# Two transformer blocks on one core: four projection chunks begin on single K tiles, group two of K is taken in two halves, and table products are merged

## The chip, the cores and the metric

The kernel runs on 1 core of a Trainium2 chip. The metric is the device time of one execution in microseconds (us). Before the change it is 1740.43 us, the median of 3 runs (1739.6 to 1742.21). The engines that matter here are TensorE (PE; its weight loads are shown apart as PEld), VectorE (DVE), ScalarE (ACT) and SyncE (SP), which issues nearly all transfers.

## The reference

Batch 1, 256 tokens, model width 2048, all in float32. Two blocks run one after the other. Only the beginning of the first concerns the change:

```
mod = silu(c) @ w_ada + b_ada                     # 2048 -> 6*2048: shift, scale, gate, twice
h   = rms_norm(x, g_attn) * (1 + sc_a) + sh_a
proj = h @ w_in                                   # 2048 -> 7632 columns, split into q, k, v, index, latent, gates
qa, ka, qi, ki, mq, mk get a rotary embedding: t1*cos - t2*sin, t2*cos + t1*sin
...                                               # sparse and dense attention, merge, gated convolution FFN
second block: pooled windows, a grouped product, a gate, an output projection, a final norm
```

Before the rotation of `qa`, `ka`, `mq` and `mk` the vectors are scaled by gains, so that the kernel folds the gains into the cosine and sine tables once.

## The kernel before

**The products.** Every large product runs in float32 split in two parts: a weight tile `raw` (512 KB, two K tiles of 128 rows by 512 columns) is loaded, ACT writes its rounded part (line 157, `SC.copy`), DVE writes the remainder (line 79, `tt(lo, src, hi, OP.subtract)`), and PE adds three products per K tile and half of the tokens (line 378): high by high, high by low, low by high. One such unit is 12 matmuls of 512 columns. There are 6 `raw` buffers (`NRAW`) and 5 split buffers `hl` (`NHL`), so that a load waits until the unit six before it has been used up.

**The modulation.** `silu(c) @ w_ada` is not a matmul: each 512 KB tile of `w_ada` is multiplied by the broadcast `c` and summed along the row on DVE (line 175, called a job here). Jobs wait in a list, and `pump(n)` emits the next n of them. A K tile of 128 rows of `h` needs four jobs (its shift and its scale, in two halves each) before its `A1` and `SH1` exist.

**The input projection** has 15 chunks of 512 columns (the first, `MISC`, of 400; `QI0`, `QI1` stay in PSUM, the `keep` tiles). Since the modulation comes tile by tile, K is cut in groups of K tiles, `groups = [(0, 2), (2, 6), (6, 10), (10, 16)]`. For each group all 15 chunks are taken in turn and added to partial sums `pacc`: copied by ACT in the first group (line 426), added by DVE later. Between two chunks the jobs of the next group are emitted at a rate of 1.05 times what is needed; three chunks before the end of a group the list is emptied up to that group (`pump_to`) and `prep1` makes the next `hT`: ACT applies scale and shift, ACT and DVE split the result.

**The head** (lines 289 to 340) is written in a `manual_schedule`, that is, its instructions stand on each engine in the order of the code: load `c` and the four `xT`, squares of `xT` and their folds, the inverse root, its broadcast `rB0`, 30 small matmuls without use (`warm`), all 8 jobs of the first group, the split of the first weight unit, `prep1(0)`, the other three `xT` norms. What comes after the head is put in order by the scheduler of the framework; each engine then works its list strictly in that order.

**The tables** (lines 448 to 490): some twenty small DVE operations on the angles `ang`, two sines on ACT, and 16 products of `cs` and `sn` with the gains `grow` (`tqa`, `tka`, `tqm`, `tkm`).

Of the kernel before, what the change touches and what calls it, by code (L numbers as in the profile page):

```python
# [29 lines left out]
def block_pair_kernel(ctx: ExitStack, tc: tile.TileContext, T: dict, out: bass.AP):  # L30
# [187 lines left out]
    def job_group(g):  # L218
        k0, k1 = groups[g]
# [40 lines left out]
    def prep1(g):  # L260
        k0, k1 = groups[g]
# [27 lines left out]
    with tc.manual_schedule(engines={ET.SP, ET.DVE, ET.Activation, ET.PE}):  # L289
# [29 lines left out]
        job_group(0)  # L319
# [18 lines left out]
        prep1(0)  # L338
# [27 lines left out]
    def gemm_gen(st, W, k0, nk, evac, rate=0.0, tail=0, head=0, kw=None, n=512, pre=(), ps=None,  # L366
# [32 lines left out]
        for a in late:  # L399
# [5 lines left out]
    w1 = {i: (T["w_misc"] if i == MISC else T["w_in"][i - 1]) for i in range(15)}  # L405
    n1 = {i: (NMISC if i == MISC else 512) for i in range(15)}
    acc = {}

    keep = {QI0: [ps_tp([128, 512], name="keep") for _ in range(2)],
            QI1: [ps_at([128, 512], name="keep") for _ in range(2)]}  # L410
    for i in range(7):
        if i not in keep:
            acc[i] = s4([128, 2, 512], name=f"pacc{i}")
# [20 lines left out]
    for g in range(1, NG + 1):  # L434
        job_group(g)
    for g in range(NG):
        k0, k1 = groups[g]
        for i in range(nch[g]):
            if g == 0 and i >= 7:
                acc[i] = s4([128, 2, 512], name=f"pacc{i}")  # L440
            gemm(st1, w1[i], k0, k1 - k0, evac1(i, g), n=n1[i], rate=rates[g],
                 pre=[unit0] if g == 0 and i == MISC else [], ps=keep.get(i), part=(g == 0 or i not in keep, i not in keep))
            if i == nch[g] - 3:
                pump_to(4 * sum(size[g + 2:]))
                prep1(g + 1)
        if g == 0:
# [35 lines left out]
            def folded(o, n, f0, name):  # L482

                r = const([128, 4, 2, n], name=name)
                for q, (tab, go) in enumerate(((cs, 0), (sn, n), (cs, n), (sn, 0))):
                    gb = grow[:, None, o + go:o + go + n].to_broadcast([128, 2, n])
                    tt(r[:, q], tab[:, :, f0:f0 + n], gb, OP.mult)
                return r
            tqa, tka = folded(0, 16, 0, "tqa"), folded(32, 16, 0, "tka")
            tqm, tkm = folded(64, 32, 24, "tqm"), folded(128, 32, 24, "tkm")  # L490
# [189 lines left out]
    def rope_a(a, H, tab):  # L680
        v = heads(a, H)
        rope(v[:, :, :, 0:16], v[:, :, :, 16:32], [tab[:, q] for q in range(4)], H, 16)
# [115 lines left out]
    rope(kr[:, :, :, 0:32], kr[:, :, :, 32:64], [tkm[:, q] for q in range(4)], 1, 32)  # L798
# [7 lines left out]
    for j in range(4):  # L806
        qv = mq[j].rearrange("p t (h d) -> p t h d", d=192)
        kv = mkv[j].rearrange("p t (h d) -> p t h d", d=256)
        rope(qv[:, :, :, 128:160], qv[:, :, :, 160:192], [tqm[:, q] for q in range(4)], 2, 32)
# [496 lines left out]
```

## Time and profile before

| | |
|---|---|
| Median of 3 runs | 1740.43 us |
| The profiled execution | 1743.09 us, its span 1741.3 us |
| PE busy | 1692.9 us, 97% of the span |
| DVE busy | 1369.1 us, 79% |
| ACT busy | 910.8 us, 52% |
| Granted TensorE clock, mean | 0.989 of full speed |
| DMA | 455.59 MB, mean 262 GB/s |
| `raw` from `w_ada`, `w_in`: issue to landing, median | 4.8, 5.1 us |

Busy time of PE says only that a matmul was under way; how many it finished is read from the counts. The share over the whole span hides the beginning: PE has its gaps there, and from about 96 us on there are hardly any until the end of the projection. So the stretches of the first 165 us are read one by one: first PE's gaps, then, for each gap, what the engine before it was doing and for whom that one waited.

### The profile page before, as it was taken

The numbers are of one execution on the slowest core, as the hardware profiler recorded it, in microseconds if no ns is written. First come the engines' busy times: TensorE is split into PE (matmuls) and PEld (weight loads), VectorE is DVE, ScalarE is ACT, GpSimd is POOL, SyncE is SP. The second block draws the span as 40 slices with busy tenths as digits, with TensorE's granted clock in tenths as the row PEclk, the third lists the DMA queues.
The fourth block names the chain that finished last, engine by engine and source line by source line (L and its number), as shares of the span: only waits on it lengthen the run. The fifth ranks groups of instructions, "written<-read, shape, count | busy, mean of one in ns | idle before, by whom it ended". The sixth has DMA issues, their size and how long they took to land.

```text
span 1741.3 us, 22010 instructions
## 1 busy us (share of the span) xinstructions
PE 1692.9 (97%) x7786; PEld 1385.5 (80%) x7786; DVE 1369.1 (79%) x2079; ACT 910.8 (52%) x1283; POOL 4.2 (0%) x15
## 2 busy tenths in 40 slices
PE   8899999999999989999999999999999999999997
PEld 6688888878778868788888788887888777888886
DVE  8899999998978767599677676777877777766765
ACT  4644354767854456555455544555345565454443
POOL 0000000000000000000000000000000000000000
PEclk9999999999999999999999999999999999999999
DMA  8999988588868868677877787777777748778762
GB/s 324 342 333 324 339 324 278 191 295 295 277 224 323 287 206 313 214 242 238 296 247 251 232 268 261 260 245 261 272 255 252 248 160 269 255 254 277 238 201 94
DMA packets 127495, 455.59 MB, mean 262 GB/s; under 512 B 14357, under 2 KB 15893, under 8 KB 127385
## 3 DMA queue, kind: packets, MB, share of 16 engines
q1 hardware_dynamic: 127384, 454.19, 77.0%
q8 instruction: 61, 1.00, 0.2%
q14 instruction: 50, 0.40, 0.1%
HBM read 452.04 MB, written 2.10 MB: 261 GB/s over the span
## 4 chain that ended last, share of the span: by engine, by line
PE 59%; DMA 18%; DVE 14%; issue 5%; ACT 3%; SPq 0%; DVEq 0%; ACTq 0%
PE mm L378 51%; DMA raw<-in_w_mod 13%; DVE hl L79 5%; DMA raw<-in_w_ada 4%; DVE raw L175 3%; PE keep L378 2%; ACT hl L157 1%; PE mm L1171 1%; DVE cv L1031 1%; PE tp L1025 1%; DVE score L599 1%; DVE cv L1033 0%; DVE pacc L79 0%; PE tp L922 0%; DMA cst<-in_cst 0%
## 5 line engine op out<-in xcount | busy, mean ns | idle before, releaser
L157 ACT CAST hl<-raw 128x1024 fp32r<-128x1024 f32 (+2 forms) x564 | 586.6, 1046 | 584.5 <-PE mm L378 432.0
L79 DVE TENSOR_TENSOR hl<-raw,hl 128x1024 fp32r<-128x1024 f32 (+2 forms) x564 | 675.7, 1212 | 141.5 <-ACT hl L157 140.8
L378 PE MATMUL mm<-hl,hN 128*128 128x512 f32 x2880 | 676.4, 394 | 6.6 <-DVE hN L79 2.4
L378 PEld LDWEIGHTS mm<-hl,hN 128*128 128x128 f32 x2880 | 540.8, 190 | 121.3 <-DVE hN L79 4.0
L175 DVE SCALAR_TENSOR_TENSOR raw<-raw,cB 128x1024 f32<-128x1024 f32 x288 | 350.5, 1220 | 184.7 <-DMA raw<-in_w_mod 139.9
L378 PE MATMUL mm<-hl,hT 128*128 128x512 f32 (+1 forms) x1248 | 290.9, 392 | 8.0 <-ACT hT L157 3.3
L378 PEld LDWEIGHTS mm<-hl,hT 128*128 128x128 f32 x1248 | 234.2, 190 | 56.5 <-ACT hl L157 4.1
L378 PE MATMUL mm<-hl,gThi 128*128 128x512 f32 x704 | 219.9, 395 | 6.2 <-DVE hl L79 3.4
L378 PEld LDWEIGHTS mm<-hl,gThi 128*128 128x128 f32 x704 | 132.9, 190 | 35.9 <-DVE hl L79 5.0
L378 PE MATMUL mm<-hl,gTlo 128*128 128x512 f32 x352 | 137.8, 395 | 0.0
L378 PE MATMUL mm<-hl,pair 128*128 128x512 f32 x384 | 89.5, 392 | 0.0
L378 PE MATMUL mm<-hl,zT 128*128 128x512 f32 x384 | 87.5, 389 | 0.0
L378 PEld LDWEIGHTS mm<-hl,zT 128*128 128x128 f32 x384 | 71.9, 188 | 14.8
L378 PEld LDWEIGHTS mm<-hl,pair 128*128 128x128 f32 x384 | 71.5, 188 | 14.6
L378 PEld LDWEIGHTS mm<-hl,gTlo 128*128 128x128 f32 x352 | 66.9, 190 | 13.8 <-DVE gTlo L79 0.2
L1029 ACT ACTIVATE cv<-tp,wcv 128x256 f32<-128x256 f32 x88 | 44.9, 562 | 47.9 <-DVE cv L1033 39.4
L79 DVE TENSOR_TENSOR pacc<-pacc,mm 128x512 f32<-128x512 f32 (+1 forms) x78 | 52.2, 671 | 6.8 <-PE mm L378 6.3
L378 PE MATMUL mm<-hl,oaT 128*128 128x512 f32 x192 | 48.0, 399 | 0.0
L378 PE MATMUL mm<-hl,obT 128*128 128x512 f32 x192 | 47.1, 397 | 0.6 <-DVE obT L79 0.6
L378 PE MATMUL keep<-hl,hT 128*128 128x512 f32 x192 | 45.7, 395 | 0.8 <-DVE hl L79 0.8
L378 PEld LDWEIGHTS keep<-hl,hT 128*128 128x128 f32 x192 | 36.5, 191 | 9.0 <-DVE hl L79 1.6
L378 PEld LDWEIGHTS mm<-hl,obT 128*128 128x128 f32 x192 | 35.1, 188 | 8.0 <-DVE obT L79 1.0
(331 smaller groups left out, 1191.1 us busy)
## 6 DMA issues: line engine op xcount, KB each, us to landing
raw<-in_w_ada SPq DMA_DIRECT2D x192, 512.0 KB, 4.8
raw<-in_w_up SPq DMA_DIRECT2D x176, 512.0 KB, 4.6
raw<-in_w_in SPq DMA_DIRECT2D x112, 512.0 KB, 5.1
raw<-in_w_mod SPq DMA_DIRECT2D x96, 512.0 KB, 4.5
raw<-in_w_down SPq DMA_DIRECT2D x88, 512.0 KB, 4.6
raw<-in_pool_w_in SPq DMA_DIRECT2D x64, 512.0 KB, 4.5
raw<-in_w_o SPq DMA_DIRECT2D x32, 512.0 KB, 4.9
raw<-in_pool_w_out SPq DMA_DIRECT2D x32, 512.0 KB, 4.3
```

Source lines behind the costliest of these rows:

```text
L79: return V.tensor_tensor(o, a, b, op=op)
L157: SC.copy(hi, src)
L175: V.scalar_tensor_tensor(raw, raw, 1.0, cact[cv][h], op0=OP.mult, op1=OP.mult, accum_out=acc)
L378: PE.matmul(ps[t][:, :n], lhsT=st(k0 + k, t, a), rhs=hl[b][:, i, :], start=(part[0] and k == 0 and x == 0), stop=(part[1] and k == nk - 1 ...
L599: V.scalar_tensor_tensor(score, r[:, i, :], w, score, op0=OP.mult, op1=OP.add)
L1025: PE.transpose(p[:, i, t * 128:(t + 1) * 128], u[:, t, f * 128:(f + 1) * 128], ident)
L1029: SC.activation(cv[:, f, :], p[:, i, :], AF.Identity, bias=wcv[:, 3, fi:fi + 1], scale=wcv[:, 2, fi:fi + 1])
L1031: V.scalar_tensor_tensor(cv[:, f, 1:], p[:, i, :255], wcv[:, 1, fi:fi + 1], cv[:, f, 1:], op0=OP.mult, op1=OP.add)
L1171: PE.matmul(pv[:, q, :], lhsT=hls[k // 2][wa][:, k % 2, f * 128:(f + 1) * 128], rhs=pooled[i][xb][:, k, :], start=(k == 0 and x == 0), sto ...
```

## The change

- **Head, order of loads.** The first K group, tiles (0, 2), is taken tile by tile by the chunks 0 to 3. Four jobs (tile 0) are emitted, then half of the first weight unit is loaded (`load_half`, 205 or 262 KB, each in a `raw` buffer of its own), `hT` is made for one tile (`prep_half`), and 6 matmuls follow (`mm_half`), the same for chunk 1, two jobs, chunks 2 and 3, two jobs; then the second tile with its four halves. The four chunks hold their PSUM tiles meanwhile (two pairs of `mm`, two of `keep`). ACT copies the sums of chunk 0 between the matmuls of chunk 0 and the split for chunk 1. `colB`, `grow`, `posi` and `wcv` are loaded after all eight halves.
- **Second group in halves.** Jobs of tiles (2, 4) and (4, 6) are separate groups, with a `fin` (four small DVE operations) each. Chunks 4 to 14 take K tiles (0, 2) as before, with 1.53 jobs per unit; then chunks 0 to 3 take (2, 4) with their sums kept in PSUM, `prep1(4, 6)`, the same chunks take (4, 6) in the order 0, 3, 1, 2, and chunks 4 to 14 take (2, 6).
- **Tables.** The 16 products become 4, of 128 and 256 columns.
- **Squares.** The squares of `xT[0]` and `xT[2]` go from DVE to ACT.

```diff
-        q[0]()
-        tt(xsq[0], xT[0], xT[0], OP.mult)
-        fold(0)
-        SC.activation(xsq[1], xT[1], AF.Square)
...
+        for c in range(3):
+            q[c]()
+            SC.activation(xsq[c], xT[c], AF.Square)
+            fold(c)
...
-        job_group(0)
+        for k in range(2):
+            job_group(k, k + 1)
         pump(WU[0])
...
         warm(ones, WU[1])
-        pump(WU[2])
+        pump(1)
         norm_x(0)
-        pump(WU[3])
-        unit0 = load_split(T["w_misc"][0], NMISC)
-        pump(1000)
+        pump(2)
...
+        def load_half(c, i):
+            n = n1[c]
+            raw = raw_tile()
+            nc.sync.dma_start(raw[:, :n], w1[c][0][:, i * n:(i + 1) * n])
...
+            split(hl0[c][:, 0, i, :n], hl0[c][:, 1, i, :n], raw[:, :n])
...
+        load_half(0, 0)
+        prep_half(0)
+        mm_half(0, 0)
+        load_half(1, 0)
+        mm_half(1, 0)
+        pump(2)
+        for c in range(2, 4):
+            load_half(c, 0)
+            mm_half(c, 0)
+        pump(2)
+        load_half(0, 1)
+        prep_half(1)
...
+        for c in range(4):
+            if c > 0:
+                load_half(c, 1)
+            mm_half(c, 1)
+            if c not in keep:
+                for t in range(2):
+                    SC.copy(acc[c][:, t, :n1[c]], ps0[c][t][:, :n1[c]])
         nc.sync.dma_start(colB, T["pcol"][:, 48:COL_N])
...
-        prep1(0)
...
-    for g in range(1, NG + 1):
-        job_group(g)
+
+    for k0, k1 in ((2, 4), (4, 6), *groups[2:]):
+        job_group(k0, k1)
+    rates[0] = RG * 4 * size[1] / (nch[0] - 4)
...
+        if g == 1:
...
+            for i in range(4):
+                gemm(st1, w1[i], 2, 2, lambda t, p: None, n=n1[i], rate=rates[1], ps=ps1[i], part=(i not in keep, False))
+            prep1(4, 6)
+            for i in (0, 3, 1, 2):
+                gemm(st1, w1[i], 4, 2, evac1(i, 1), n=n1[i], rate=rates[1], ps=ps1[i], part=(False, i not in keep))
+        for i in range(done, nch[g]):
```

**What stands where now.** On ACT before, in the second half of the first group: `hl_450` is the split of the unit after the chunk whose sums are in `mm_418`, `mm_419`.

```order
L157 CAST hl_422<-raw_420 128x1024
L426 COPY pacc_72_392<-mm_393 128x512
L426 COPY pacc_72_392<-mm_394 128x512
L426 COPY pacc_78_417<-mm_418 128x512
L426 COPY pacc_78_417<-mm_419 128x512
L157 CAST hl_450<-raw_448 128x1024
L157 CAST hl_475<-raw_473 128x1024
```

The split `hl_450` stands behind the copy of the sums of the chunk just before it; `hl_475` stands ahead of the copies of its own predecessor. On ACT after, in the same part of the program (`hl_498`, `hl_551` and `hl_595` are the units of the chunks summed in `mm_494`, `mm_547` and the next):

```order
L457 COPY pacc_88_460<-mm_461 128x512
L457 COPY pacc_88_460<-mm_462 128x512
L157 CAST hl_498<-raw_496 128x1024
L255 ACTIVATE h_119_585<-xT_92,SH_74,A_73 128x256 x2
L157 CAST hl_523<-raw_521 128x1024
L457 COPY pacc_96_493<-mm_494 128x512
L457 COPY pacc_96_493<-mm_495 128x512
L457 COPY pacc_102_518<-mm_519 128x512
L457 COPY pacc_102_518<-mm_520 128x512
L157 CAST hl_551<-raw_549 128x1024
L457 COPY pacc_109_546<-mm_547 128x512
L157 CAST hT_584<-h_119_585 128x512
```

Two splits in these rows stand behind the copies of the chunk just before them, and two rows further on `hl_595` does, behind the copy of `mm_548`. On DVE before, between the third last and the second last unit of the first group (`raw`, `vs` are jobs; `SH`, `A` the shift and scale made from them):

```order
L79 TENSOR_TENSOR hl_525<-raw_523,hl_525 128x1024
L175 SCALAR_TENSOR_TENSOR raw_540,vs_250<-raw_540,cB_83 128x1024
L175 SCALAR_TENSOR_TENSOR raw_545,vs_250<-raw_545,cB_82 128x1024
L175 SCALAR_TENSOR_TENSOR raw_548,vs_250<-raw_548,cB_83 128x1024
L79 TENSOR_TENSOR vs_250<-vs_250 128x8
L79 TENSOR_TENSOR SH_74<-vs_250,colA 128x4
L79 TENSOR_TENSOR A_73<-vs_250,colA 128x4
L226 SCALAR_TENSOR_TENSOR A_73<-A_73,colA 128x4
L79 TENSOR_TENSOR hl_572<-raw_570,hl_572 128x1024
```

Three jobs and four small operations stand between two splits. On DVE after, the end of the same stretch (`hl_551` stands three jobs ahead of the first row; `ang` and `angk` belong to the tables, and `hl_595` is the second last unit):

```order
L79 TENSOR_TENSOR hT_584<-h_119_585,hT_584 128x512
L175 SCALAR_TENSOR_TENSOR raw_577,vs_487<-raw_577,cB_83 128x1024
L512 SCALAR_TENSOR_TENSOR ang_648<-angkh_650,ang_648 128x112
L79 TENSOR_TENSOR vs_487<-vs_487 128x4
L513 SCALAR_TENSOR_TENSOR ang_648<-angk_649,ang_648 128x112
L79 TENSOR_TENSOR SH_74<-vs_487,colA 128x2
L79 TENSOR_TENSOR A_73<-vs_487,colA 128x2
L512 SCALAR_TENSOR_TENSOR ang_648<-angkh_650,ang_648 128x112
L225 SCALAR_TENSOR_TENSOR A_73<-A_73,colA 128x2
L513 SCALAR_TENSOR_TENSOR ang_648<-angk_649,ang_648 128x112
L515 TENSOR_SCALAR ang_648<-ang_648 128x112
L79 TENSOR_TENSOR hl_595<-raw_593,hl_595 128x1024
```

Four jobs, one `hT` and nine small operations now stand between two splits, and the table operations, which stood in the second group, stand here.

## Rows read from the trace of the kernel before

**Rows 1.** The page, busy time of engines (share of the span, instructions).
```profile
PE 1692.9 (97%) x7786; PEld 1385.5 (80%) x7786; DVE 1369.1 (79%) x2079; ACT 910.8 (52%) x1283; POOL 4.2 (0%) x15
```
**Rows 2.** Busy time by windows: PE, PEld, DVE, ACT, POOL, then PEclk, DMA share, GB/s.
```profile
20.00:40.00 20.00, 16.73 (x86) 14.81 (x85) 19.36 (x32) 7.01 (x10) 0.00 (x0) 0.83 0.90 306
...
80.00:100.00 20.00, 19.18 (x87) 15.60 (x86) 19.93 (x50) 10.10 (x12) 0.00 (x0) 1.00 0.91 324
100.00:120.00 20.00, 20.00 (x90) 16.57 (x89) 19.24 (x27) 9.48 (x9) 0.00 (x0) 1.00 0.94 349
```
**Rows 3.** Timeline of the head: start, us, engine, line, operation.
```profile
10.14 0.23 DVE L448 CAST identb<-cst 128x128 bf16<-128x128 f32 x1 [0.44 <-DMA cst<-in_cst]
...
12.40 1.22 DVE L175 SCALAR_TENSOR_TENSOR raw<-raw,cB 128x1024 f32<-128x1024 f32 x1
...
15.16 1.22 DVE L175 SCALAR_TENSOR_TENSOR raw<-raw,cB 128x1024 f32<-128x1024 f32 x1
...
15.78 8.74 PE L112 MATMUL warm<-ones 128*128 128x128 f32 x60
...
25.33 0.16 DVE L79 TENSOR_TENSOR vs<-vs 128x4 f32<-128x4 f32 x1
...
25.99 1.09 ACT L256 ACTIVATE h<-xT,SH,A 128x256 f32<-128x256 f32 x2 [6.39 <-DVE A L226]
...
27.79 4.43 PE L378 MATMUL mm<-hl,hT 128*128 128x400 f32 x12 [3.27 <-ACT hT L157]
```
**Rows 4.** Half-microsecond windows, columns as in rows 2: the granted clock falls and rises.
```profile
26.50:27.00 0.50, 0.00 (x0) 0.00 (x0) 0.50 (x1) 0.50 (x2) 0.00 (x0) 0.53 0.98 401
...
33.00:33.50 0.50, 0.50 (x3) 0.40 (x2) 0.50 (x1) 0.47 (x1) 0.00 (x0) 0.64 0.22 90
```
**Rows 5.** The same windows around 57 us.
```profile
57.00:57.50 0.50, 0.20 (x1) 0.00 (x0) 0.50 (x1) 0.36 (x1) 0.00 (x0) 0.75 0.92 377
...
60.50:61.00 0.50, 0.50 (x3) 0.43 (x2) 0.50 (x1) 0.35 (x1) 0.00 (x0) 0.83 1.05 197
```
**Rows 6.** Timeline, the gap of PE near 55 us.
```profile
54.88 0.58 ACT L426 COPY pacc<-mm 128x512 f32<-128x512 f32 x1 [0.55 <-PE mm L378]
55.37 2.00 ACT L157 CAST hl<-raw 128x1024 fp32r<-128x1024 f32 x2
56.45 1.22 DVE L79 TENSOR_TENSOR hl<-raw,hl 128x1024 fp32r<-128x1024 f32 x1 [1.92 <-ACT hl L157]
...
57.73 12.07 PE L378 MATMUL mm<-hl,hT 128*128 128x512 f32 x46 [0.52 <-DVE hl L79]
```
**Rows 7.** The chain that ended last: start, us, engine and tile.
```profile
10.36 0.61 DVE xsq L79
11.00 1.04 DVE xsq L79 x2
...
15.24 2.29 DVE raw L175 x4
```
**Rows 8.** The chain from 160 us on.
```profile
165.21 10.92 PE keep L378 x48
176.13 71.76 PE mm L378 x324
```
**Rows 9.** Groups of the first 100 us by form: busy, mean ns, idle before.
```profile
L157 ACT CAST hl<-raw 128x1024 fp32r<-128x1024 f32 x22 | 23.0, 1049 | 10.2 <-DMA raw<-in_w_in 10.2
...
L471 DVE SCALAR_TENSOR_TENSOR ang<-angkh,ang 128x112 f32<-128x112 f32 x4 | 1.1, 271 | 0.0
...
L79 DVE TENSOR_TENSOR tqm<-sn,grow 128x64 f32<-128x64 f32 x2 | 0.3, 216 | 0.0
...
L79 DVE TENSOR_TENSOR tqa<-sn,grow 128x32 f32<-128x32 f32 x2 | 0.3, 181 | 0.0
```
**Rows 10.** Tile `raw`, transfers of the first 110 us.
```profile
DMA to landing us min/median/max: 3.6/5.1/8.9
```
**Rows 11.** Transfers of the first 100 us: KB each, median us to landing.
```profile
posi<-in_positions SPq DMA_DIRECT2D x1, 1.0 KB, 5.8
```

More of the change, by code (lines that the diff above doesn't have):

```diff
@@ L328, in block_pair_kernel, with prep_half, mm_half @@
         warm(ones, WU[1])
-        pump(WU[2])
+        pump(1)
         norm_x(0)
-        pump(WU[3])
-        unit0 = load_split(T["w_misc"][0], NMISC)
-        pump(1000)
+        pump(2)
+        w1 = {i: (T["w_misc"] if i == MISC else T["w_in"][i - 1]) for i in range(15)}
+        n1 = {i: (NMISC if i == MISC else 512) for i in range(15)}
+        keep = {QI0: [ps_tp([128, 512], name="keep") for _ in range(2)],
+                QI1: [ps_at([128, 512], name="keep") for _ in range(2)]}
+        ps0 = {i: keep.get(i) or [ps_mm(), ps_mm()] for i in range(4)}
+        hl0 = {}
+        hT[0] = s4([128, 2, 2, 256], F32R, name="hT")
+        def load_half(c, i):
+            n = n1[c]
+            raw = raw_tile()
+            nc.sync.dma_start(raw[:, :n], w1[c][0][:, i * n:(i + 1) * n])
+            if i == 0:
+                n_s4[0] += 1
+                hl0[c] = sp.tile([128, 2, KT, 512], F32R, name=f"hl_{n_s4[0]}", tag="hl", bufs=NHL)
+            split(hl0[c][:, 0, i, :n], hl0[c][:, 1, i, :n], raw[:, :n])
+        def prep_half(i):
+            h = t2([128, 256], name="h32")
+            SC.activation(h, xT[0][:, i, :], AF.Identity, scale=A1[:, i:i + 1], bias=SH1[:, i:i + 1])
+            split(hT[0][:, 0, i, :], hT[0][:, 1, i, :], h)
+        def mm_half(c, i):
+            n = n1[c]
+            for t in range(2):
+                for x, (a, b) in enumerate(((0, 0), (0, 1), (1, 0))):
+                    PE.matmul(ps0[c][t][:, :n], lhsT=hT[0][:, a, i, t * 128:(t + 1) * 128], rhs=hl0[c][:, b, i, :n],
+                              start=(i == 0 and x == 0), stop=(i == 1 and x == 2 and c not in keep))
+        load_half(0, 0)
[10 more added lines that the diff above has]
+        prep_half(1)
+        acc = {i: s4([128, 2, 512], name=f"pacc{i}") for i in range(7) if i not in keep}
+        for c in range(4):
[3 more added lines that the diff above has]
+            if c not in keep:
+                for t in range(2):
+                    SC.copy(acc[c][:, t, :n1[c]], ps0[c][t][:, :n1[c]])
         nc.sync.dma_start(colB, T["pcol"][:, 48:COL_N])
@@ L402, in gemm_gen @@
         yield
[L405 to L413, printed above, removed]
     st1 = st_pairs(hT)
@@ L433, in block_pair_kernel @@
     rates = [RG * 8 * size[g + 1] / (nch[g] * size[g]) for g in range(NG)]
-    for g in range(1, NG + 1):
-        job_group(g)
+    for k0, k1 in ((2, 4), (4, 6), *groups[2:]):
+        job_group(k0, k1)
+    rates[0] = RG * 4 * size[1] / (nch[0] - 4)
     for g in range(NG):
         k0, k1 = groups[g]
-        for i in range(nch[g]):
+        done = 4 if g < 2 else 0
+        if g == 1:
+            ps1 = {i: keep.get(i) or [ps_mm(), ps_mm()] for i in range(4)}
+            for i in range(4):
[4 more added lines that the diff above has]
+        for i in range(done, nch[g]):
             if g == 0 and i >= 7:
@@ L441, in block_pair_kernel @@
             gemm(st1, w1[i], k0, k1 - k0, evac1(i, g), n=n1[i], rate=rates[g],
-                 pre=[unit0] if g == 0 and i == MISC else [], ps=keep.get(i), part=(g == 0 or i not in keep, i not in keep))
+                 ps=keep.get(i), part=(g == 0 or i not in keep, i not in keep))
             if i == nch[g] - 3:
                 pump_to(4 * sum(size[g + 2:]))
-                prep1(g + 1)
+                prep1(*((2, 4) if g == 0 else groups[g + 1]))
         if g == 0:
@@ L681, in rope_a @@
         v = heads(a, H)
-        rope(v[:, :, :, 0:16], v[:, :, :, 16:32], [tab[:, q] for q in range(4)], H, 16)
+        rope(v[:, :, :, 0:16], v[:, :, :, 16:32], tab, H, 16)
     rope_a(acc[KV], 2, tka)
@@ L797, in block_pair_kernel @@
     kr = misc[:, :, None, 336:400]
-    rope(kr[:, :, :, 0:32], kr[:, :, :, 32:64], [tkm[:, q] for q in range(4)], 1, 32)
+    rope(kr[:, :, :, 0:32], kr[:, :, :, 32:64], tkm, 1, 32)
     causb = const([128, 128], BF16, name="causb")
```

27 lines of the change are left out of this document (10 added, 17 removed).

## The prediction

> **What bounds the kernel now.** The page comes first: PE is under way for 97% of the span [rows 1], so that a change pays only where PE waits or runs at half clock. The windows show where: from 20 to 40 us the granted clock is 0.83 and PE's busy time 16.73 of 20 us, from 80 to 100 us there are still small gaps, and from 100 us on PE is full at clock 1.00 [rows 2]. The chain gives the full pace: 48 matmuls of 512 columns in 10.92 us, 0.2274 each; 324 matmuls, 36 of them of 400 columns, in 71.76 us, so 0.174 for one of 400 [rows 8]. The first keep matmul of the third group starts at 165.21; the 24 matmuls of MISC before it take 4.2, so the second group ends at 161.0. Up to there PE has 540 matmuls, 36 of 400 columns: 120.9 us of work. PE is therefore 40.1 us late by then, and all of the change lies in these 161 us. I follow this lateness: time minus work done.
>
> Its first piece is the start: first matmul at 27.79 [rows 3]; PE had finished the warm matmuls at 24.5, the clock fell to half at 26.5 and rose again at 33.3 [rows 4]. Half speed from 27.79 to 33.3 costs 2.75, so the lateness is 30.5 there. The other 9.6 come in gaps. The one at 55 us shows how: ACT copies the sums of a chunk (54.88), only then splits the next unit (55.37), DVE makes its low part (56.45), and PE goes on at 57.73 [rows 6]. Gap 2.8 less two matmuls in it, 2.4. It is an effect of ACT's list, not of a late transfer. After it the clock falls too, from 57.2 to 60.7 [rows 5]: 1.5 more.
>
> **The change, step by step.** Each engine works its list in order, so I take the new lists and add durations: a job on DVE 1.145 from start to start (two in 2.29 [rows 7]), the low part of a whole unit the same (both are 1.22 busy [rows 3, 6]), of half a unit 0.61 like the fold of 512 columns [rows 7], 0.48 for 400 columns; four small operations 0.66 (25.33 to 25.99 [rows 3]); a split on ACT about 1.0 [rows 6, 9]; a table operation on `ang` 0.3 or a little less [rows 9].
>
> *Start.* The squares moved to ACT relieve DVE by 2.4, but DVE then waits for `cst`, which lands at 10.14: the cast of `identb` now stands behind the first fold, and three folds of 1.04 instead of two follow it. Everything behind comes 1.05 later: the second job at 16.2 instead of 15.16, the warm matmuls from 16.83 to 25.57 instead of from 15.78 [rows 3, 7]. DVE does two jobs less before the first `A1`, and two norms and jobs and the small operations end at 21.6, `hT` stands at 22.6. But PE is still busy with the warm matmuls until 25.57. So the first matmul comes 2.2 earlier, not 5, and as PE was never idle the clock need not fall: lead 2.2 + 2.75 = 4.95.
>
> *Second halves.* DVE's list: `hT` low part and half a unit, two jobs, two halves, two jobs, four small ones, half of MISC: 22.65 + 0.4 + 0.61 + 2.29 + 1.22 + 2.29 + 0.15 of waits + 0.66 + 0.48 = 30.8. Next stands the memset on `colB`, which was loaded long before; now its load is issued behind all half loads, the last of which gets its buffer at 27.3, so at 27.8. Its landing isn't shown for a short queue. The nearest rows are 3.6 for the shortest `raw` transfer [rows 10] and 5.8 for `posi` in the same place of the queue with more ahead of it [rows 11]: 31.4 to 33.6. I take 31.8, near the lower, since fewer bytes are outstanding. `hT`'s low part would end at 31.65 anyway and now does at 32.2, so the stall costs 0.6, between 0.2 and 2.0.
> The Trainium skill, page "DMA: Bandwidth & Descriptors", section "Anatomy of one DMA — SWDGE (gpsimd) path", puts a transfer at a fixed 2.0 us plus its bytes by 436 GB/s. By that, as an estimate, `colB` would land at 29.8 and DVE would not wait at all; the sum below would be 3.9 instead of 4.5. The 3.6 for 512 KB is close to the page's 3.2, the 5.8 for 1 KB is not; the queue ahead makes the difference, and no row shows one without a queue.
>
> PE finishes both halves of MISC at 33.05. ACT's list has the two copies of it (0.5 each) before the split for chunk 1, so this half is split at 34.1 and its low part done at 34.8; two more halves to 36.0, the three `xT` norms (1.145 each), and the first whole unit is ready at 40.6. PE has done 52 matmuls by then, 10.5 us of work: lateness 30.1. The lead of 4.95 over the old 30.5 at this point has shrunk to 0.4.
>
> *To the end of the first group.* DVE now sets the pace. From 40.6 it has 12 jobs and 8 low parts (22.9), four small operations (0.66), nine table operations (2.7) until the third last unit: 66.9. Two waits for ACT come on top, where a split stands behind the copies of the chunk just before it (0.7 and 1.1): 68.7. There PE loses 0.9 near 52 us, 2.3 near 58 and 2.7 near 66, each the pattern of rows 6. The unit is through at 71.0. Until the next low part DVE has four jobs (4.58), `hT` (0.6), nine small operations, of which four belong to the now separate tiles (4, 6) and five to the tables (2.1), and the low part itself: 77.2. PE idles from 71.0 on but for two matmuls, 5.8 lost. Then two jobs, two angles, two merged table products, one low part: 81.9, 2.0 lost. Then a job, two table products, MISC's low part (0.9), a job, `hT`, a low part: 87.5, 0.9 lost. From here DVE hands over a unit at least every 2.3 us, and PE needs 2.73, so PE is full. In sum the losses are 14.6: lateness 44.7.
>
> *The tables.* From 32 to 64 columns a product grows from 0.181 to 0.216 [rows 9], 1.1 ns a column: 0.29 and 0.43 for 128 and 256. Four make 1.4 where sixteen made 3.2. This is in the sums above (0.7 a pair), and would be worth 1.8 at most, had the products stayed in the second group.
>
> *The transfers.* A buffer is used up some 7 us after it was issued, six units of DVE work, against 5.1 to landing [rows 10]; I add nothing. With landings near the 8.9 of the same row, one or two splits would come about 1 us later.
>
> *The sum.* From 87.5 PE has 346 matmuls left, 12 of 400 columns: 76.0 + 2.1, end at 165.6 instead of 161.0: +4.5. Behind it PE is as full as before, so the delay goes through to the end. The profiled execution took 1743.09 (span 1741.3): 1747.6. It stood 2.66 above the median; against the median 1740.43 that is 1744.9, so I say 1745. With the bounds of `colB` (-0.4 to +1.4), half a microsecond of error in each of four gaps and later landings, this case itself reaches from 1742 to 1748.
>
> **The rivals.**
> *The lead is kept (faster).* If PE loses no more between 40 and 90 us than it does now, 9.6, the 4.95 of the start remain: 1735.5. For it speaks that the first matmul does come earlier and without the half-clock stretch. Against it speak the lists: the three norms, the small operations of two more groups and the tables stand before low parts that PE waits for. It decides from the point where the second last unit of the first group is ready before about 71 us rather than at 77.
> *Nothing changes.* The stage ends when DVE has done its work, whatever the order: 2.4 less for squares, 1.8 less for tables, 1.3 more for two more `fin`, 0.4 more for halves, 2.5 less in all: 1738. For it: DVE is busy 19.9 of 20 us from 80 to 100 [rows 2]. Against: PE is the full one from 96 us on, so DVE's total is not what ends the stage.
> *The clock falls in the new gaps (slower still).* After the gap near 55 us it fell for 3.4 us, cost 1.5 [rows 5, 6]. Four gaps of this kind stand in the new stretch; in the longest it hides behind DVE, in two or three it adds 1 to 1.5: 1748. The Trainium skill, "TensorE: Matmul & The Clock Gate", section "Why this matters for your kernels", warns against idle gaps between bursts for this reason; rows 4 and 5 agree with it.
>
> **The chances.** Forecast 0.48, lead kept 0.18, nothing changes 0.20, clock 0.14. What a measurement of this kernel can tell from no change is about 0.2%, 3.5 us: the line is at 1743.9. Of the forecast a quarter lies below it: slower 0.36 + 0.14 = 0.50, same 0.12 + 0.20 = 0.32, faster 0.18. The range takes in the clock case and most of the faster one: 1736.5 to 1750.
>
> **What would show it.** First matmul at 25.6 with the clock at 1.00 from 20 to 40 us; DVE waiting at the memset of line 490 for `colB` near 31 us; ACT's split for chunk 1 behind the copies of line 374; the first whole low part near 40.6; a gap of PE of about 6 us before the second last unit, near 71 to 77; the third group starting 4 to 5 us later than 161.0. I am wrong if PE has no gap above 3 us between 57 and 82, or if the third group starts before 161 us.

## The result and the profile after

| | before | after |
|---|---|---|
| Median of the runs | 1739.73 us (1739.38 to 1742.21) | 1750.44 us (1744.97 to 1752.91) |
| The profiled execution, its span | 1743.09, 1741.3 us | 1752.91, 1751.1 us |
| First projection matmul | 27.79 us | 25.06 us |
| Group three's first `keep` matmul | 165.05 us | 174.14 us |
| First `dots` matmul (end of the projection) | 277.23 us | 286.32 us |

The changed kernel is slower: ratio 1.0054, 95% interval 1.004 to 1.0069, so 7 to 12 us. (A seventh run of the changed kernel, disturbed, took 3422.89 us; it is left out of all these figures, and with it the median would be 1751.29 us.) The whole difference is there at 174 us: 9.1 us later than before, still 9.1 at the first `dots`, 9.8 at the end. I call the start of group three's matmuls on the kept banks *the mark*; it is the best reading of what an edit does to the first two groups, since the total scatters by some microseconds from run to run. It says nothing of what comes after it.

Page and windows of the changed kernel, which answer to [rows 1, 2] (the windows' columns are those of rows 2):

```profile
PE 1694.6 (97%) x7786; PEld 1385.5 (79%) x7786; DVE 1369.8 (78%) x2078; ACT 914.0 (52%) x1290; POOL 5.2 (0%) x15
```
```profile
20.00:40.00 20.00, 16.32 (x84) 13.44 (x84) 14.65 (x33) 8.73 (x15) 0.00 (x0) 0.85 0.84 263
80.00:100.00 20.00, 18.07 (x73) 14.49 (x74) 17.82 (x28) 12.77 (x18) 0.00 (x0) 0.91 0.93 343
100.00:120.00 20.00, 20.00 (x92) 16.84 (x91) 17.11 (x22) 8.77 (x9) 0.00 (x0) 1.00 0.89 311
```

The page hides the loss: PE's share is 97% in both. The windows show it: 73 matmuls from 80 to 100 us where there were 87, at clock 0.91 in place of 1.00. From 100 us on PE is full again.

PE's timeline of the changed kernel (start, us, engine, line, operation, in brackets the idle time before and what ended it):

```profile
16.58 8.72 PE L112 MATMUL warm<-ones 128*128 128x128 f32 x60
25.06 1.34 PE L353 MATMUL mm<-hl,hT 128*128 128x400 f32 x6
...
33.07 1.68 PE L353 MATMUL mm<-hl,hT 128*128 128x400 f32 x6 [2.58 <-ACT hT L157]
35.85 5.53 PE L353 MATMUL keep<-hl,hT 128*128 128x512 f32 x12 [1.10 <-ACT hl L157]
...
42.58 11.59 PE L418 MATMUL mm<-hl,hT 128*128 128x512 f32 x48
...
62.60 0.73 PE L418 MATMUL mm<-hl,hT 128*128 128x512 f32 x2 [1.62 <-ACT hl L157]
63.86 6.90 PE L418 MATMUL mm<-hl,hT 128*128 128x512 f32 x22 [0.52 <-DVE hl L79]
72.38 0.73 PE L418 MATMUL mm<-hl,hT 128*128 128x512 f32 x2 [1.62 <-ACT hl L157]
...
77.82 0.73 PE L418 MATMUL mm<-hl,hT 128*128 128x512 f32 x2 [1.62 <-ACT hl L157]
81.34 4.61 PE L418 MATMUL mm<-hl,hT 128*128 128x512 f32 x12 [2.79 <-DVE hl L79]
```

The warm matmuls run into the first half chunks without a gap, as predicted. Then the pattern of [rows 6], a split behind copies that wait for PE, comes at 62.6, 72.4 and 77.8. All idle times from 42.58 to 92 us add to 10 us, and matmuls are slow after them: 22 in 6.90 us, 12 in 4.61, where the full pace is 5.0 and 2.7. The clock fell three times where it had fallen twice before [rows 4, 5]:

```profile
36.00:40.00 4.00, 4.00 (x9) 2.88 (x10) 4.00 (x6) 2.83 (x4) 0.00 (x0) 0.50 0.92 313
64.00:68.00 4.00, 4.00 (x12) 3.12 (x13) 3.93 (x9) 1.35 (x3) 0.00 (x0) 0.61 0.86 263
80.00:84.00 4.00, 2.66 (x7) 2.13 (x8) 4.00 (x9) 3.01 (x6) 0.00 (x0) 0.74 0.89 343
```

In the first two rows `PE` is "busy" for 4.00 us with 9 and 12 matmuls where the full pace gives 18: a busy PE at a lower clock, half of it in the first row.

VectorE, low parts of whole units in the first group, changed kernel (the first one, the four that waited by 73.5 us, and the second last):

```profile
41.04 1.22 DVE L79 TENSOR_TENSOR hl<-raw,hl 128x1024 fp32r<-128x1024 f32 x1
...
50.07 1.23 DVE L79 TENSOR_TENSOR hl<-raw,hl 128x1024 fp32r<-128x1024 f32 x1 [0.96 <-ACT hl L157]
54.38 1.23 DVE L79 TENSOR_TENSOR hl<-raw,hl 128x1024 fp32r<-128x1024 f32 x1 [0.79 <-ACT hl L157]
...
62.58 1.22 DVE L79 TENSOR_TENSOR hl<-raw,hl 128x1024 fp32r<-128x1024 f32 x1 [1.71 <-ACT hl L157]
...
72.36 1.23 DVE L79 TENSOR_TENSOR hl<-raw,hl 128x1024 fp32r<-128x1024 f32 x1 [1.51 <-ACT hl L157]
80.07 1.22 DVE L79 TENSOR_TENSOR hl<-raw,hl 128x1024 fp32r<-128x1024 f32 x1
```

And the head, where the prediction had its stalls:

```profile
28.73 0.42 SPq L375 DMA_DIRECT2D colB<-in_pcol  x1
...
30.06 1.23 DVE L175 SCALAR_TENSOR_TENSOR raw<-raw,cB 128x1024 f32<-128x1024 f32 x1 [1.71 <-DMA raw<-in_w_ada]
30.50 0.53 ACT L157 CAST hl<-raw 128x400 fp32r<-128x400 f32 x1 [6.18 <-DMA raw<-in_w_misc]
...
32.72 0.06 DVE L490 MEMSET colB<- 32x2 f32 x1 [0.28 <-DMA colB<-in_pcol]
...
34.01 0.49 ACT L374 COPY pacc<-mm 128x400 f32<-128x400 f32 x1 [1.00 <-PE mm L353]
```

A job came 1.71 us late, the memset waited for `colB` (landed 4.0 us after its issue), the copy of MISC's sums waited for PE ahead of the next split. From 42 to 92 us it is the order that shows, not a late transfer: VectorE's waits are for ScalarE's split (5.5 us in five), and ScalarE's split waits for a load once, 0.34 us.

### The profile page after: what moved, and what is told of

Its sections match the earlier page's. It is cut to its first block, busy times and chain, and to the rows that moved or that the text cites. A ratio compares the mean times of both kernels' runs of the same rounds, so it can differ in the third digit from the quotient of the medians.

```text
span 1751.1 us, 22014 instructions
## 1 busy us (share of the span) xinstructions
PE 1694.6 (97%) x7786; PEld 1385.5 (79%) x7786; DVE 1369.8 (78%) x2078; ACT 914.0 (52%) x1290; POOL 5.2 (0%) x15
## 4 chain that ended last, share of the span: by engine, by line
PE 50%; DMA 19%; DVE 14%; issue 14%; ACT 2%; SPq 0%; DVEq 0%; POOL 0%; ACTq 0%; POOLq 0%
PE mm L418 44%; DMA raw<-in_w_mod 13%; DVE hl L79 6%; DMA raw<-in_w_ada 4%; DVE raw L175 3%; ACT hl L157 1%; PE mm L1212 1%; PE tp L1066 1%; PE keep L418 1%; DVE cv L1072 1%; DMA raw<-in_w_up 1%; DVE pacc L79 0%; DVE cv L1074 0%; PE tp L1179 0%; DVE score L640 0%
## 5 line engine op out<-in xcount | busy, mean ns | idle before, releaser
L157 ACT CAST hl<-raw 128x1024 fp32r<-128x1024 f32 (+3 forms) x568 | 587.2, 1040 | 588.6 <-PE mm L418 423.7
L79 DVE TENSOR_TENSOR hl<-raw,hl 128x1024 fp32r<-128x1024 f32 (+3 forms) x568 | 676.9, 1206 | 142.5 <-ACT hl L157 141.6
L418 PE MATMUL mm<-hl,hT 128*128 128x512 f32 (+1 forms) x1224 | 286.9, 393 | 9.8 <-ACT hl L157 5.1
L418 PEld LDWEIGHTS mm<-hl,hT 128*128 128x128 f32 x1224 | 229.6, 190 | 59.2 <-DVE hl L79 7.2
L418 PE MATMUL mm<-hl,zT 128*128 128x512 f32 x384 | 87.5, 389 | 0.0
L418 PEld LDWEIGHTS mm<-hl,oaT 128*128 128x128 f32 x192 | 35.9, 193 | 7.4 <-issue 0.2
L418 PE MATMUL keep<-hl,hT 128*128 128x512 f32 x168 | 39.2, 391 | 0.3 <-DVE hl L79 0.3
```

The lines of the kernel that those rows point to most:

```text
L79: return V.tensor_tensor(o, a, b, op=op)
L157: SC.copy(hi, src)
L418: PE.matmul(ps[t][:, :n], lhsT=st(k0 + k, t, a), rhs=hl[b][:, i, :], start=(part[0] and k == 0 and x == 0), stop=(part[1] and k == nk - 1 ...
```

## The experiments

Twelve kernels, each with its mark (one profiled execution) and its time against the kernel before on the same chip. In these sessions the kernel before had medians of 1739.1 to 1741.0 us, but single runs from 1732 to 1750, so a ratio is good to about 0.002.

| kernel | mark | median, us | ratio to before, interval |
|---|---|---|---|
| before | 165.05 | 1739.73 | 1 |
| the changed kernel | 174.14 | 1750.44 | 1.0054, 1.004 to 1.0069 |
| e14: before, tables | 164.41 | 1740.95 | 1.001, 0.999 to 1.003 |
| e1: before, tables and squares | 166.06 | 1743.67 | 1.0018, 1.0004 to 1.0033 |
| e3: before, second group in halves | 165.47 | 1744.08 | 1.002, 1.0003 to 1.0037 |
| e8: before, splits ahead | 168.29 | 1744.54 | 1.002, 1.0003 to 1.0037 |
| e11: before, more buffers | 212.73 | 1797.48 | 1.0325, 1.0289 to 1.0361 |
| e2: changed, second group whole | 173.07 | 1756.38 | 1.0082, 1.0059 to 1.0104 |
| e4: changed, head's orders | 172.85 | 1750.81 | 1.0058, 1.0037 to 1.0079 |
| e5: changed, splits ahead | 172.23 | 1757.07 | 1.0087, 1.0065 to 1.0109 |
| e7: changed, seven buffers | 171.63 | 1748.50 | 1.0041, 1.0027 to 1.0055 |
| e9: changed, clock kept up | 173.74 | 1753.22 | 1.0071, 1.0048 to 1.0094 |
| e10: changed, own buffers | 174.06 | 1752.53 | 1.007, 1.0042 to 1.0098 |
| e16: e10, jobs spread | 162.63 | 1744.86 | 1.0036, 1.002 to 1.0052 |

The mark and the time do not always agree: e2 and e5 have their marks 1.1 and 1.9 us before that of the changed kernel and ratios 0.003 above its own, 5 to 6 us. In e5 the loss is seen between the first `dots` and the first `gThi` matmul (539.5 us in place of 534.1 in the profiled executions), where nothing was edited; why is open.

### Which part of the change costs (e1, e14, e2, e3)

**e1, tables and squares alone**, on the kernel before:

```diff
-        tt(xsq[0], xT[0], xT[0], OP.mult)
...
+            SC.activation(xsq[c], xT[c], AF.Square)
...
-            tqa, tka = folded(0, 16, 0, "tqa"), folded(32, 16, 0, "tka")
+            tqa, tka = folded(0, 16, 0, "tA")
```

> The kernel before with the two small parts of the change alone: the two squares on ScalarE and the four table operations in the place of sixteen; the first chunks and the second group stay as they were. Theory A (the first four chunks taken tile by tile are the whole loss): these parts are worth nothing to a small gain, 1737.5 to 1740.5 us, because the 1.8 us that VectorE saves on the tables lie in the first group, where TensorE waits for VectorE's low parts. Rival B (the tables, now read through wide broadcasts, and the reordered list of VectorE around them cost a good part of it): 1743 or more.

**e14, the tables alone** (the squares as before):

> The kernel before with the four table operations in the place of sixteen and nothing else; the two squares stay on VectorE. If the 3 us of the run with tables and squares come from the squares (VectorE's first job 0.8 us later, every raw buffer freed that much later): 1739 to 1741 us here. If they come from the tables and the order around them: 1742 to 1745 us.

The tables cost nothing (1.001, 0.999 to 1.003). Their products stand in the second group in e1 and e14 (at 90.7 to 94.8 us), not in the first as the expectation of e1 has it, so they are off the stretch in which PE waits. e1's 1743.67 us is the number of rival B, but its cause falls with e14; what is left are the squares, with a mark 1.6 us later than with the tables alone (the two times do not tell them apart). In e1's profile the first projection matmul is at 31.61 us, 3.8 later than before, since two jobs waited 1.1 and 1.2 us for their loads, and the mark is only 1.0 later. So a late start is mostly given back. That was the first sign that the start is not what the mark hangs on.

**e2, the second group whole again**, on the changed kernel:

```diff
-    for k0, k1 in ((2, 4), (4, 6), *groups[2:]):
+    for k0, k1 in groups[1:]:
...
-        done = 4 if g < 2 else 0
-        if g == 1:
...
+        done = 4 if g == 0 else 0
```

> The changed kernel with the second group put back to whole chunks (jobs of tiles 2 to 5 as one set, all of hT for them prepared at once); the first four chunks stay tile by tile. Theory A: the loss is in the first chunks, 1748 to 1753 us, and group three starts its matmuls on the kept banks near 174 us as in the changed kernel. Rival C (the second group in halves, its extra accumulations and the way its jobs are spread, is where most is lost): 1739 to 1743 us, group three near 166 us.

**e3, the second group in halves alone**, on the kernel before:

```diff
+        done = 4 if g == 1 else 0
+        if g == 1:
...
+            prep1(4, 6)
...
-                prep1(g + 1)
+                prep1(*((2, 4) if g == 0 else groups[g + 1]))
```

> The kernel before with the second group's first four chunks in two halves (tiles 2 and 3, then 4 and 5) and the jobs in two sets; the first group stays as before. Theory A: no loss, 1736 to 1741 us; a gain of 0 to 3 us where hT for the second group waits for fewer jobs. Rival C: 1746 us or more.

The loss goes with the new first group (e2: mark 173.07, its time above even theory A's numbers), not with the halves (e3: mark 165.47; its time, 0.5 to 6.4 us over the kernel before, lies between the theories). But "the new first group" is two things: four chunks taken tile by tile, and the sixteen jobs of the second group put into the eleven chunks that are left, 1.53 each, where fifteen chunks had 1.12. e2 has both, e3 neither.

### Is it the head? (e4, e7, e9, e10)

**e4, the head's orders**: copies behind all splits, small loads early.

```diff
+        nc.sync.dma_start(colB, T["pcol"][:, 48:COL_N])
...
         load_half(0, 1)
         prep_half(1)
...
             mm_half(c, 1)
+        for c in range(4):
             if c not in keep:
```

> The changed kernel with two orders mended: the copies of MISC's and Q0's sums out of PSUM stand behind all four second-half splits on ScalarE (not between the first and the second), and colB, grow, posi and wcv are issued before the second halves, so that VectorE's memset and cast no longer wait for them. Theory D (the lists of ScalarE and VectorE in the head carry the loss: 1.0 us of ScalarE waiting for TensorE, 1.6 us of copies, 0.6 us of VectorE waiting for colB and posi): 1747.5 to 1749.5 us, the first whole low part (41.04 us in the changed kernel) 2 to 3 us sooner. Rival E (the stretches at half clock and the late transfers carry it, the order nothing): 1750 to 1752 us with the clock still near 0.5 from 34 to 41 us.

**e7, seven raw buffers**: `NS4, NRAW, NHL = 27, 7, 5` in place of `28, 6, 5`.

> The changed kernel with seven raw buffers in the place of six (and 27 in the place of 28 of the larger shared ones, to make room). Rival H (each half-size load holds a whole buffer, so that fewer bytes are under way: 230 GB/s from 20 to 30 us, where the kernel before moved 323): the rate of that stretch rises to about 280 GB/s, the job that came 1.7 us late at 30 us is on time, total 1745 to 1749 us. Theory G: the rate may rise, but the gaps behind the copies stay: 1749.5 to 1752 us.

PE of e7, where the pattern comes at the same three places, 2.5 us earlier each:

```profile
41.02 17.44 PE L418 MATMUL mm<-hl,hT 128*128 128x512 f32 x72
60.08 0.73 PE L418 MATMUL mm<-hl,hT 128*128 128x512 f32 x2 [1.62 <-ACT hl L157]
...
69.85 0.73 PE L418 MATMUL mm<-hl,hT 128*128 128x512 f32 x2 [1.62 <-ACT hl L157]
...
75.30 0.73 PE L418 MATMUL mm<-hl,hT 128*128 128x512 f32 x2 [1.62 <-ACT hl L157]
```

**e9, PE kept busy** in the gap before the second halves:

```diff
+        def fill_pe(n):
+            for _ in range(n):
+                PE.matmul(ps0[MISC][0][:, NMISC:], lhsT=ones, rhs=ones[:, :512 - NMISC], start=False, stop=False)
+        fill_pe(9)
         load_half(0, 1)
```

> The changed kernel with nine small matmuls (112 columns, into spare columns of MISC's bank that nothing reads) in TensorE's gap between the first and the second halves, 30.5 to 33.07 us. Theory I (that gap made the clock fall from 34.2 to 41.0 us, and the half clock costs 3 to 4 us that are kept to the end): clock 1.00 there, 41 us reached with the second halves done by 39 us, total 1747 to 1749 us. Against it (the 3 us at half clock lie beside VectorE's 41.04 us for the first whole low part, so nothing is won): clock 1.00, but the first whole chunk starts at 42 us all the same, total 1750 to 1752 us. If the clock falls in spite of busy matmuls, the gap is not its cause.

**e10, own buffers for the half loads**:

```diff
+            r = s4([128, 512], name="rawh")
...
+        late = {c: dma_half(c, 1) for c in range(4)}
         load_half(0, 1)
```

> The changed kernel with the eight half-size loads of the head in buffers of their own (eight of the larger shared ones that are free there; the four second halves are issued together where the first of them stood), so that the six raw buffers serve the jobs and the whole chunks alone. The lists of ScalarE, VectorE and TensorE stay as they are but for three small places. Rival H (the half-size loads, each holding a whole raw buffer, starve the queue: from 10 to 30 us the changed kernel moved 533 x 10 us x GB/s where the kernel before moved 699, and what is not moved there is missing until 90 us): more than 600 from 10 to 30 us, no wait of VectorE for a job near 30 us, second halves in without waiting, group three near 168 to 171 us, total 1742 to 1747 us. Rival J (the loss is in the work of the engines, the two dozen small instructions of the head and TensorE's two gaps, the supply being a result of it): transfers earlier, total still 1749 to 1752 us.

e4, e9 and e10 did in the head what they were built for. First window of the changed kernel, then of e10 (transfers from 10 to 30 us), then e9 (clock, 36 to 40 us, 0.50 in the changed kernel):

```profile
10.00:30.00 20.00, 17.27 (x99) 16.38 (x100) 16.93 (x38) 5.96 (x11) 0.00 (x0) 1.00 0.79 266
```
```profile
10.00:30.00 20.00, 17.27 (x98) 16.46 (x99) 18.48 (x43) 6.45 (x12) 0.00 (x0) 1.00 1.02 386
```
```profile
36.00:40.00 4.00, 3.85 (x17) 3.20 (x18) 4.00 (x6) 2.03 (x3) 0.00 (x0) 1.00 0.96 335
```

PE reaches its first whole chunk at 39.31 (e4), 40.15 (e9) and 38.70 us (e10) in place of 42.58: 2.4 to 3.9 us won. At the mark 1.3, 0.4 and 0.1 of it are left, and no time is gained. So half clock in the head (e9), the copies and `colB` (e4) and the late transfer (e10) each cost time where they stand, at most 1.3 us of it reaches the mark, and none the time; they were taken away one by one, not together. Theories D and I, as causes of the loss, fall. The advice of the Trainium skill, "TensorE: Matmul & The Clock Gate", section "Why this matters for your kernels", to leave no idle gaps between bursts is borne out on the clock by e9, but the clock was not what bound.

Rival H, the supply, fares less clearly. e7's 1748.50 us and its punctual job (28.47 us, no wait) are what H said; its rate from 20 to 30 us, 244 GB/s, is hardly above the 230 of the changed kernel, and its gaps behind copies stay, as theory G said. It starts its whole chunks 1.6 us earlier (41.02) and has won 2.5 at the mark, the one head start that was not lost; its interval overlaps that of the changed kernel. e10 goes against H, but its supply has a hole later (0 GB/s from 36 to 40 us), so that from 10 to 100 us it moves the same 311 GB/s as the changed kernel. That the hole is not what took e10's lead is shown by e16 below, which has the same hole.

### What takes the head start (e5, e8, e11, e16)

e10's PE between 40 and 81 us shows where its 3.9 us go:

```profile
53.28 0.73 PE L424 MATMUL mm<-hl,hT 128*128 128x512 f32 x2 [1.62 <-ACT hl L157]
54.53 6.92 PE L424 MATMUL mm<-hl,hT 128*128 128x512 f32 x22 [0.52 <-DVE hl L79]
63.07 0.73 PE L424 MATMUL mm<-hl,hT 128*128 128x512 f32 x2 [1.62 <-ACT hl L157]
...
71.46 0.73 PE L424 MATMUL mm<-hl,hT 128*128 128x512 f32 x2 [1.62 <-ACT hl L157]
...
78.43 0.73 PE L424 MATMUL mm<-hl,hT 128*128 128x512 f32 x2 [1.62 <-ACT hl L157]
80.80 10.16 PE L424 MATMUL mm<-hl,hT 128*128 128x512 f32 x34 [1.64 <-DVE hl L79]
```

An earlier PE meets the same splits behind the same copies.

**e5 and e8, every split one chunk ahead of the copies**, on the changed kernel and (with its `unit0`) on the kernel before:

```diff
+        with tc.manual_schedule(engines={ET.Activation, ET.DVE}) if g == 0 else nullcontext():
...
+                if g == 0:
+                    cur = load_split(w1[4][0], 512) if i == 4 else nxt
+                    nxt = load_split(w1[i + 1][0], n1[i + 1]) if i < 14 else None
```

> The changed kernel with the first group from its fifth chunk on written one chunk ahead: each chunk's load, its split on ScalarE and its low part on VectorE stand before the copies out of PSUM of the chunk two before it, and both engines keep that order (in the changed kernel ScalarE does up to four copies, each waiting for TensorE, before the next split). Theory G (from 42 to 92 us the splits that stand behind copies starve TensorE, about 2.15 us at each of 62, 72 and 77 us, and the clock falls after them): the gaps that ScalarE's cast ends go, group three starts near 169 to 171 us in place of 174.1, total 1745 to 1748 us. Rival H (what bounds these 50 us is the supply, the transfers and their six buffers; the order only shows it): the gaps stay in size, with DMA as what ends them, total 1750 to 1753 us.

> The kernel before with the same edit in its first group (each split one chunk ahead of the copies, ScalarE and VectorE in that order); nothing of the change is in it. Theory G: its two starved places (54.8 to 57.7 us and 69.9 to 72.7 us) and the stretch at half clock after the first go, 2.9 plus 1.7 plus 2.8 us at most, with part of it taken by the next limit: 1734 to 1738 us. Rival H: 1739 to 1742 us.

Theory G falls in this form: e5's 1757.07 us is above the numbers of both theories, and e8's 1744.54 as well. In e5 PE has no wait above 0.8 us from 40.9 to 69.9 us, but then:

```profile
76.20 1.22 PE L418 MATMUL mm<-hl,hT 128*128 128x512 f32 x2 [2.55 <-ACT hl L157]
79.41 4.14 PE L418 MATMUL mm<-hl,hT 128*128 128x512 f32 x10 [1.99 <-DVE hl L79]
```

The first of these waits is for a load: with no copies ahead of it, the split that ends it waits 2.69 us for its weights. ScalarE's waits for loads of `w_in` in e5, from 36 to 92 us (in all, times, the longest):

```profile
ACT hl L157 <- DMA raw<-in_w_in: 7.0, 5, 2.7
```

In front of the second stand the last of the sixteen jobs, the small operations and `hT` on VectorE, since all these jobs still have to be done before `hT` of the second group. So once the order is mended, the supply that rival H spoke of and VectorE's work show in its place. e8 turns two gaps of 2.9 us into one of 5.91 us before 76.8 and has its mark 3.2 later (its profiled execution stood 9 us above its median, so this mark is worth less). The order shifts the gaps; it does not make the work less.

**e11, the weights of the first group in the larger shared buffers**, on the kernel before:

```diff
+        raw = s4([128, 1024], name="raww") if g1[0] else raw_tile()
```

> The kernel before with the weights of the first group in the larger shared buffers, so that its six raw buffers serve the jobs alone and more loads can be under way. Rival H, taken to the kernel before (its shares of 0.82 to 0.98 from 20 to 90 us would be a limit of buffers, not of the transfers): the 0.82 from 30 to 40 us rises, waits of ScalarE for raw (7.4 us from 36 to 92 us) go, total 1735 to 1738 us. If the transfers themselves are the limit there (share near 1): 1739 to 1742 us.

Far from both theories: 1797 us. From 84 us on each chunk's split runs directly behind the copies of the chunk before it, and a chunk takes about 7 us, with the granted clock at 0.67 to 0.81 (windows of 10 us from 80 to 110 us):

```profile
92.29 0.73 PE L380 MATMUL mm<-hl,hT 128*128 128x512 f32 x2 [1.62 <-ACT hl L157]
93.55 4.13 PE L380 MATMUL mm<-hl,hT 128*128 128x512 f32 x10 [0.52 <-DVE hl L79]
99.30 0.73 PE L380 MATMUL mm<-hl,hT 128*128 128x512 f32 x2 [1.62 <-ACT hl L157]
```

Loads are not its limit there: it moves 2 GB/s from 90 to 100 us. It prices the pattern, with the lower clock that comes with it: 7 us in place of 2.73 for a chunk. Why the scheduler came to this order in e11 is not shown.

**e16, the pace of the jobs**, on e10 (the rates are jobs per unit):

```diff
-    rates[0] = RG * 4 * size[1] / (nch[0] - 4)
+    rates[0] = 1.1
...
-                gemm(st1, w1[i], 2, 2, lambda t, p: None, n=n1[i], rate=rates[1], ps=ps1[i], part=(i not in keep, False))
+                gemm(st1, w1[i], 2, 2, lambda t, p: None, n=n1[i], rate=1.05, ps=ps1[i], part=(i not in keep, False))
+            pump_to(4 * sum(size[2:]))
             prep1(4, 6)
...
-                pump_to(4 * sum(size[g + 2:]))
+                pump_to(4 * sum(size[g + 2:]) + (8 if g == 0 else 0))
```

> The changed kernel with the head's half-size loads in buffers of their own, as in the run before (which ended the head 3.9 us sooner and had lost it again by 54 us), and one thing more: the second group's jobs spread, 1.1 of them a chunk in the first group's eleven whole chunks in place of 1.53 (only the eight of tiles 2 and 3 must be done by the third-last chunk), the rest at 1.05 a chunk in the second group's first four half chunks. Against the run before, this is the pace of the jobs alone. Theory K (sixteen jobs in eleven chunks are more loads and more of VectorE than a chunk's 2.73 us of TensorE covers, and the order then puts one split behind four copies at three places: the gaps of 2.15 us near 62, 71 and 78 us and the half clock after them come of it): most of these gaps go, group three starts at 164 to 168 us in place of 174.1, total 1738 to 1744 us. Against it (the loss is fixed in the head, or the transfers are the limit at any pace): the lead is lost again, group three at 172 us or later, 1748 us or more.

PE of e16 in the same stretch:

```profile
40.28 25.32 PE L424 MATMUL mm<-hl,hT 128*128 128x512 f32 x108 [1.17 <-ACT hl L157]
65.93 2.60 PE L424 MATMUL mm<-hl,hT 128*128 128x512 f32 x10 [0.33 <-DVE hl L79]
70.15 0.73 PE L424 MATMUL mm<-hl,hT 128*128 128x512 f32 x2 [1.62 <-ACT hl L157]
...
87.47 5.22 PE L424 MATMUL mm<-hl,hT 128*128 128x400 f32 x24 [1.77 <-ACT hT L157]
```
```profile
58.00:92.00 34.00, 29.11 (x125) 22.31 (x124) 32.67 (x66) 22.38 (x32) 0.00 (x0) 1.00 0.94 340
```

Against e10 the edit changes the pace alone, and 108 matmuls run from 40.28 us without a wait, one gap behind copies is left of four, the clock is 1.00 from 24 to 92 us, and the mark goes from 174.06 to 162.63 us, 2.4 before that of the kernel before. Theory K's mark came out even earlier than expected. The time fell short of it: 1744.86 us, 3.5 to 9 us slower than before.

Why the pace matters so much can be estimated from rows of this case. At 1.53 jobs a chunk, VectorE has 2.53 operations of 1.145 us to do, 2.9 us, and the queue 2.53 loads of 512 KB, which would take 486 GB/s, while PE needs 2.73 us; the best 4 us of the changed kernel (52 to 56 us) moved 420 GB/s. At 1.1 jobs it is 2.4 us and 403 GB/s. Neither e10 nor e5 takes any of this away; e16 does (17 jobs on VectorE from 38.7 to 92 us, where e10 has 20). Three things are not separated: VectorE's work, the loads, and ScalarE's order, which the scheduler changed with the pace (in e10 three splits stand behind four copies each, in e16 up to 64 us most stand between the two copies of a chunk). e5 shows that an order without copies ahead is not enough at the old pace; no run has the new pace with the old order, or without e10's buffers.

What it lost again lies in the third group. The first transposes of `kidup`, which close it, are at 264.11 us before, 273.12 in e10, 268.15 in e16. PE of the kernel before does this group without a wait; e16's waits for low parts, as from 220 to 240 us (before, then e16):

```profile
220.00:240.00 20.00, 20.00 (x90) 16.57 (x89) 18.89 (x29) 12.16 (x18) 0.31 (x1) 1.00 0.79 272
```
```profile
220.00:240.00 20.00, 18.18 (x76) 13.58 (x75) 18.13 (x28) 13.00 (x18) 0.31 (x1) 1.00 0.79 279
```

PE is now ahead of what VectorE and the transfers supply, and the jobs that were put off are late: those of the third K group are summed up (`vs`) at 144.3 us where the kernel before has 137.1, those of the fourth at 230.4 where it has 224.4. Whether that is owed to the transfers is open: e10 and e16 have a hole in them (139 GB/s from 32 to 36 us and 0 from 36 to 40 in e16; no load is issued between 29.5 and 40.2), and by 100 us e16 has moved about 1 MB less than the kernel before. No run took the hole away. In the medians e16 is 6 us behind the kernel before, and 4 of them are there at the first `dots` (281.27 against 277.23 us). That the two profiled executions end level (spans 1740.6 and 1741.3) is chance: the one stands 2.5 us below its median, the other 3.4 above. No version here beats the kernel before.

## Why the prediction was right, and where it was not

The sign was right, and the rival of a kept lead was wrong. The size was half: 1745 forecast, 1750.4 measured (the mean of the same six runs is 1749.6), outside the case's own 1742 to 1748 and at the upper end of the range, 1750; the loss at the end of group two was 9.1 us in place of 4.5. By the steps:

- *Start.* Right. First matmul at 25.06 (25.57 forecast), no gap after the warm matmuls, clock 1.00 from 20 to 32 us. The reason that "the clock need not fall" held for the start only: after the gap of 2.58 us at 30.5 it was 0.50 from 36 to 40 us, which the sum left out.
- *Second halves.* Right in the two waits that it named, the memset for `colB` and the split behind MISC's copies. The memset came at 32.72, after a wait of 0.28 us (0.6 forecast); `colB` landed 4.0 us after its issue, as taken. The sum in the Trainium skill, "DMA: Bandwidth & Descriptors", section "Anatomy of one DMA — SWDGE (gpsimd) path", gives some 2.2 us for its 77 KB, as an estimate, but that section is on transfers issued from GpSimd, and SyncE issued this one; the measurement decides. The transfers, at which it said "I add nothing", added 1.7 at the last job, and MISC's second half (from 33.07) took 1.68 us where the first took 1.34, the clock falling at 34 us. The first whole low part ended at 42.2 in place of 40.6: +1.6.
- *To the end of the first group.* This is the step that failed in size: "Two waits for ACT come on top (0.7 and 1.1)". There were four by 73.5 us, 0.96, 0.79, 1.71 and 1.51, together 4.97 in place of 1.8. With the 1.6 that makes the third-last low part 4.8 us late, and the next ones, forecast at 77.2, 81.9 and 87.5, ended at 81.2, 86.1 and 91.6: 4.0 to 4.2 late, nearly all of the 4.6 by which the mark missed. The cause is a loop that the sum of durations cut open: VectorE waits for ScalarE's split, the split for the copies ahead of it, the copies for PE, and PE, at half clock after two of its gaps (64 to 68 and 80 to 84 us), for VectorE.
- *What sets the size.* The prediction let the lateness of the head add to that of the gaps. In e4, e9 and e10 it does not: 2.4 to 3.9 us won before 43 us leave 0.1 to 1.3 (e7, with a seventh buffer all the way, is the exception: 1.6 grew to 2.5). e16 shows what does, on e10: the 1.53 jobs a chunk. The prediction had that pace in its list of VectorE's work (12 jobs and 8 low parts) but took it for a fixed cost, where it is the part of the change that makes the gaps.
- *Its sign of being wrong.* "I am wrong if PE has no gap above 3 us between 57 and 82": taken by the letter, this came true, the longest single wait being 2.79 us. What the sum meant, PE idle but for two matmuls before the second last unit, was there: from 76.20 to 81.34 us, 4.4 us of it idle (71.0 to 77.2 forecast, 5.8 lost). The sign was badly worded; the mechanism that it stood for was seen.
- *Tables.* 0.29 and 0.42 us a product, as worked out (0.29 and 0.43). It put their worth at 1.8 us at most if they stayed in the second group; there (e14) no gain can be told from none.
- *The clock rival* (0.14) named the right mechanism, with four places and 1 to 1.5 us each; two such stretches in the first group were measured, beside the one in the head. It is an effect here: e16 had none of them once the gaps were gone.

## What to carry to other kernels

Where two engines feed a third through one in-order list, an earlier start is worth little (here 0 to 2.5 us at the mark) unless the pace of the stretch behind it is kept: count the loads, products and copies that fall on each unit after the change, not only those that move. When work units are taken out of a loop, whatever was spread over the loop by a rate is packed more tightly into the rest; spread it anew (e16, 11 us at the mark against e10) before judging the edit. Read an experiment at a mark shortly behind the edited stretch and at the end: an edit can win 11 us at the one and 6 at the other.

## What the runs showed of the hardware

- A gap of PE of 2.6 us (30.5 to 33.07) was followed by half clock from about 34 to 41 us; with 18 small matmul records of 112 columns in it (e9) the clock stayed at 1.00 in the windows from 32 to 40 us.
- Not every such gap is followed by a fall: in the kernel before, gaps of the same form and length (2.9 us, with two matmuls in them) ended at 57.73 and 72.67 us; the granted clock was 0.66 from 56 to 60 us after the one and 1.00 from 72 to 76 us after the other.
- Half-size loads of 256 KB landed hardly sooner than whole ones of 512 KB in the head of the changed kernel (median 5.1 us of six, 5.4 of three, loads of `w_in` up to 40 us). With each in one of six buffers the changed kernel moved 266 GB/s from 10 to 30 us; with more buffers 386 GB/s (e10), then nothing from 36 to 40 us, and the time was no better.
